# A two-layer decoder trunk: layer 0's output projection by seven products, and what makes room for it

## The chip, the core and the metric

The kernel runs on one core of a Trainium2 chip. The core has a matrix engine (TensorE, PE in the profile), a vector engine (VectorE, DVE), a scalar engine (ScalarE, ACT), GpSimd (POOL) and SyncE (SP, which here only issues transfers). Each engine works through a queue of its own in order; semaphores make one wait for another. Transfers (DMA) between DRAM and the core's memory (SBUF) are issued from the queues of SP and POOL. Matrix products collect in PSUM, eight banks of 128 partitions x 512 floats. The metric is the device time of one execution in microseconds (us).

## The reference

Two layers on x, 512 positions by 2048 channels, all in float32:

```python
for l in range(DEPTH):                                   # 2
    mod = c_act @ w_mod[l] + b_mod[l]                    # modulation: 3 x 2048 numbers
    shift, scale, gate = jnp.split(mod, 3, axis=-1)
    h = rmsnorm(x, norm_gain[l]) * (1.0 + scale) + shift
    proj = h @ w_in[l]                                   # 2048 x 7504
    ...
    y_a = sparse_attention(q_a, k_a, v_a, ...) * silu(g_a)     # 8 heads, softmax
    y_b = head_groupnorm(retention(q_b, k_b, v_b)) * silu(g_b) # 8 heads
    y = jnp.concatenate([y_a, y_b], axis=-1) @ w_out[l]        # 2048 x 2048
    x = x + gate * y
```

## The kernel before

Channels lie on the partitions: x, h and y are 16 tiles of 128 channels by 512 positions. Every float32 operand of a product is split into a high and a low part, and a product is three matmuls (high-high, high-low, low-high), in lines L390 to L398 for plain groups.

**The stream.** All products are cut into groups, and each group into chunks of 512 KB of weights: a load `wf` on SP's queue, a copy to the high part `wh` on ScalarE (L324), a subtraction to the low part `wl` on VectorE (L334), and then the chunk's matmuls. `step` (one call a chunk) issues the load five chunks ahead and the split two chunks ahead of the matmuls, then the group's `pre` work, some steps of modulation, side work of attention and retention, and the chunk's own matmuls. A scheduler then sets the order on each engine; engines and SP's queue keep that order when the kernel runs, whatever comes late.

The groups of a layer, in order: S and the indexer, VB, QK (four), QA (two), GA (two), GB (two), and the output projection. In layer 0 the projection is four plain groups OUT of 512 output channels each, eight chunks of 24 matmuls of 512 columns (`pj<-y`). Their results are evacuated by L1461 (gate times result plus x, on VectorE; x comes in by the loads `xr`), squared on ScalarE and added up on VectorE (L556, L557), since the next layer begins with a norm. The fourth group's last two chunks run by halves of the positions (`out_halves`, tiles `po`), so that the sums of squares (`prs`, L1505) and layer 1's first `h` come early.

In layer 1 the projection already runs in four groups O7 by **seven products** (L1335 to L1365): a 2 x 2 block product, of 256 channels and 256 positions a block, in seven block products instead of eight. A chunk is 42 matmuls of 256 columns. This takes sums of weight blocks (`wsum`, split into `ws` or `wsh` and `wsl`, L272 to L291) and sums of blocks of y (`put_seven`). The results `u1`, `u3`, `uc` of a group are scaled by the gate on ScalarE (L1389), then POOL adds x with an accumulating transfer (L1398) and stores the sum to the output (L1399); the fourth block goes another way (`xr`, L1404 and L1411). POOL issues them in order: accumulate, store, accumulate, store, accumulate, store.

**Modulation.** Layer 0's gate and layer 1's modulation are computed on the side (`mod_rest`), in half-tile steps: a load `mw` of 512 KB, a tiny copy on POOL from the newest `wl` (L416; it only holds the step back until that split is done), and a multiply-and-sum on VectorE (L417). Two `mw` tiles take turns. `MODN` is the number of steps a chunk in each group. Layer 1's scale and shift must be there before layer 1 begins. 96 steps lie before that.

Of the kernel before, what the change touches and what calls it, by code (L numbers as in the profile page):

```python
# [136 lines left out]
def hybrid_trunk(ctx, tc, xt, positions, wmod, w_in, w_out, cst_d, dec_d, out):  # L137
# [128 lines left out]
    def seven_hi(i):  # L266

        if "sum" not in seven:
            seven["sum"] = sm("wsum", D, tag="cb")
# [2 lines left out]
        act(h[:, :3 * QC], w[:, QC:], AF.Copy)  # L272
        tt(s[:, :2 * QC].rearrange("p (b c) -> p b c", c=QC), w[:, :QC].unsqueeze(1).to_broadcast([P, 2, QC]),
           w[:, 2 * QC:].rearrange("p (b c) -> p b c", c=QC), op=OP.subtract)
# [1 line left out]
        tt(s[:, 3 * QC:], w[:, QC:2 * QC], s[:, 2 * QC:3 * QC], op=OP.subtract)
        if i % 3 < 2:
            t = gen_mw("ws", F32R)
            pieces = [(t[:, :1024], t[:, 1024:], slice(0, 1024))]
        else:  # L280
            pieces = [(G("wsh", F32R), G("wsl", F32R), slice(n * T, (n + 1) * T)) for n in range(2)]
        for sh, _, c in pieces:
            act(sh, s[:, c], AF.Copy)
        whl[i] = h, s, pieces

    def seven_lo(i):
        h, s, pieces = whl[i]
        lo = ring.tile([P, 1024], F32R, name="wl", tag="wl")
        tt(lo[:, :3 * QC], wf.pop(i)[:, QC:], f(h[:, :3 * QC]), op=OP.subtract)
        for sh, sl, c in pieces:  # L290
            tt(sl, s[:, c], f(sh), op=OP.subtract)  # L291

        def part(q):
            if q < 3:
                return h[:, q * QC:(q + 1) * QC], lo[:, q * QC:(q + 1) * QC]
            c0 = (q - 3) * QC
            sh, sl, c = next(p for p in pieces if p[2].start <= c0 < p[2].stop)
            o = c0 - c.start
            return sh[:, o:o + QC], sl[:, o:o + QC]
# [186 lines left out]


# [456 lines left out]
    def layer(l):  # L944
# [285 lines left out]
        def att_task(h, qh, ql):  # L1230
# [48 lines left out]
            for j in range(NB):  # L1279
                v, su = Lt[j]  # L1280
                ts(v, v, su, None, op0=OP.mult)
# [109 lines left out]
        def seven_put(g, i, t, v):  # L1391
# [7 lines left out]
            (dma if g.end else nc.gpsimd.dma_start)(out=xs_of(outv, g, i, t), in_=halves(v))  # L1399

# [55 lines left out]

        def evac_out(g):
            def ev(n, ps):
                k = 4 * g + n
                t = A(k, "xn") if first else G("xo")  # L1460
                stt(t, ps, mod_col(l, 2, k), xr.pop(k), op0=OP.mult, op1=OP.add)  # L1461
                if first:
                    X[k] = t
                    if k == 0:
                        ss["t"] = G("ssq")
                    if k < KT - 4:
                        add_sq(ss["t"], t, k)
# [177 lines left out]
```

## Time and profile before

| what | value |
|---|---|
| median of 3 runs | 1850.31 us (1849.68 to 1850.46) |
| the profiled execution, its time | 1849.68 us |
| its span in the profile | 1847.9 us |
| VectorE, ScalarE busy | 1384.4 us, 888.0 us |
| layer 0's projection, first to last plain matmul and on to `po` | 783.06 to 946.33 us |
| layer 1's projection begins | 1681.14 us |
| modulation steps (L417), both layers | 132 of 1.2 to 1.5 us |

The page gives busy time, the clock that was granted to TensorE, and the chain of work that ended last. In rows of groups, the last part is the idle time of the engine just ahead of the group, and what ended it. In a timeline a row is start, duration, engine, line, operation, and in brackets the idle time before it and what ended that. Layer 0's projection lies at slices 17 to 20 of the page's 40.

### The profile page before, as it was taken

How to read it: one execution, taken by the hardware profiler on the slowest of the kernel's cores; microseconds unless marked ns; L12 is line 12 of the kernel's file. 1: busy time of each engine (PE TensorE's matmuls, PEld its weight loads, DVE VectorE, ACT ScalarE, POOL GpSimd, SP SyncE). 2: the span in 40 equal slices, each digit the busy share in tenths (PEclk: the TensorE clock that was granted, in tenths of full speed). 3: DMA queues.
4: the chain of work that ended last, by engine and by line, in shares of the span. 5: the costliest groups of instructions: out<-in, count | busy, mean ns of one | idle time of the engine just before them, and what ended most of it. 6: DMA issues, size and time to landing. Idle time of an engine off the chain costs nothing.

```text
span 1847.9 us, 26300 instructions
## 1 busy us (share of the span) xinstructions
PE 1821.7 (99%) x9644; PEld 1562.9 (85%) x9644; DVE 1384.4 (75%) x2438; ACT 888.0 (48%) x1708; POOL 70.8 (4%) x184
## 2 busy tenths in 40 slices
PE   7999999999999999999999999999999999999998
PEld 7878888888888888888899988888888888889998
DVE  7996699787867846777776699377875686369886
ACT  7668943564546532422235542344444554245443
POOL 0001000000000000100000000000000000000111
PEclk7999999999999999999999999999999999999999
DMA  9995533333454547789864323444534354333554
GB/s 371 364 321 178 165 88 92 109 114 95 123 186 123 174 147 236 233 281 308 304 208 129 103 80 100 142 124 147 155 120 124 93 185 135 102 92 109 149 151 130
DMA packets 175762, 304.55 MB, mean 165 GB/s; under 512 B 16960, under 2 KB 92864, under 8 KB 172048
## 3 DMA queue, kind: packets, MB, share of 16 engines
q1 hardware_dynamic: 171328, 295.23, 50.5%
q0 software_dynamic: 4160, 7.41, 1.6%
q8 instruction: 76, 1.25, 0.3%
q14 instruction: 54, 0.44, 0.1%
q10 hardware_dynamic: 144, 0.22, 0.0%
HBM read 289.18 MB, written 13.63 MB: 164 GB/s over the span
## 4 chain that ended last, share of the span: by engine, by line
PE 83%; DVE 2%; ACT 2%; DMA 1%; issue 1%; SPq 0%; DVEq 0%; ACTq 0%
PE pj L390 15%; PE pj L391 15%; PE pj L392 15%; PE pj L398 6%; PE pj L397 6%; PE pj L396 6%; PE p L1356 3%; PE p L1355 3%; PE p L1354 3%; PE ptr L177 1%; PE pdot L1028 1%; DVE wl L334 1%; PE pdot L1030 1%; ACT wh L324 1%; PE plg L1250 1%
## 5 line engine op out<-in xcount | busy, mean ns | idle before, releaser
L324 ACT ACTIVATE wh<-wf 128x1024 fp32r<-128x1024 f32 (+2 forms) x277 | 284.7, 1029 | 586.9 <-PE pj L391 390.1
L334 DVE TENSOR_TENSOR wl<-wf,wh 128x1024 fp32r<-128x1024 f32 (+2 forms) x277 | 326.6, 1180 | 289.1 <-ACT wh L324 282.5
L390 PE MATMUL pj<-h,wh 128*128 128x512 f32 (+1 forms) x1280 | 488.4, 382 | 1.9 <-ACT bt L911 1.7
L391 PE MATMUL pj<-h,wh 128*128 128x512 f32 (+1 forms) x1280 | 485.9, 380 | 2.6 <-DVE h L631 2.6
L392 PE MATMUL pj<-h,wl 128*128 128x512 f32 (+1 forms) x1280 | 485.7, 379 | 0.5 <-DVE wl L334 0.5
L390 PEld LDWEIGHTS pj<-h,wh 128*128 128x128 f32 x1280 | 240.6, 188 | 44.9 <-issue 2.5
L391 PEld LDWEIGHTS pj<-h,wh 128*128 128x128 f32 x1280 | 240.6, 188 | 42.1 <-DVE h L631 3.8
L392 PEld LDWEIGHTS pj<-h,wl 128*128 128x128 f32 x1280 | 240.5, 188 | 41.4 <-DVE wl L334 1.1
L396 PE MATMUL pj<-wh,h 128*128 128x512 f32 (+1 forms) x616 | 234.6, 381 | 4.1 <-ACT h L625 3.4
L397 PE MATMUL pj<-wl,h 128*128 128x512 f32 (+1 forms) x616 | 233.6, 380 | 0.7 <-DVE wl L334 0.7
L398 PE MATMUL pj<-wh,h 128*128 128x512 f32 (+1 forms) x616 | 232.6, 380 | 0.2 <-DVE h L631 0.2
L396 PEld LDWEIGHTS pj<-wh,h 128*128 128x128 f32 x616 | 116.5, 189 | 26.7 <-ACT h L625 3.9
L397 PEld LDWEIGHTS pj<-wl,h 128*128 128x128 f32 x616 | 116.5, 189 | 20.3 <-DVE wl L334 1.1
L398 PEld LDWEIGHTS pj<-wh,h 128*128 128x128 f32 x616 | 116.2, 189 | 20.4 <-DVE h L631 0.4
L417 DVE CUSTOM_DVE_ANT_0 mw<-mw,cb 128x1024 f32<-128x1024 f32 (+1 forms) x64 | 93.0, 1453 | 7.0 <-POOL mp L416 5.6
L417 DVE CUSTOM_DVE_ANT_0 mw<-mw,cb,mp 128x1024 f32<-128x1024 f32 x68 | 88.3, 1298 | 12.4 <-POOL md L416 7.9
L392 PE MATMUL pj<-y,wl 128*128 128x512 f32 x240 | 93.4, 389 | 0.0
L391 PE MATMUL pj<-y,wh 128*128 128x512 f32 x240 | 93.4, 389 | 0.0
L390 PE MATMUL pj<-y,wh 128*128 128x512 f32 x240 | 93.4, 389 | 0.0
L1262 ACT ACTIVATE bias<-bias,mx 128x128 f32<-128x128 f32 (+1 forms) x64 | 35.9, 561 | 65.3 <-DVE mx L1261 64.6
L1036 DVE SCALAR_TENSOR_TENSOR iacc<-relu,wi,iacc 128x384 f32<-128x384 f32 (+2 forms) x96 | 55.5, 613 | 10.1 <-ACT relu L1034 7.2
L894 ACT ACTIVATE ind<-pos,pt 128x512 bf16<-128x512 f32 (+3 forms) x128 | 61.4, 553 | 0.1
(549 smaller groups left out, 3077.3 us busy)
## 6 DMA issues: line engine op xcount, KB each, us to landing
wf<-in_w_in_dram SPq DMA_DIRECT2D x155, 512.0 KB, 3.7
mw<-in_wmod_dram SPq DMA_DIRECT2D x136, 512.0 KB, 5.7
wf<-in_w_in_dram SPq DMA_DIRECT2D x136, 256.0 KB, 3.1
mw<-in_wmod_dram SPq DMA_DIRECT2D x28, 1024.0 KB, 8.6
wf<-in_w_out_dram SPq DMA_DIRECT2D x32, 512.0 KB, 5.3
wf<-in_w_out_dram SPq DMA_DIRECT2D x64, 256.0 KB, 3.5
dec<-in_decay_dram SPq DMA_DIRECT2D x32, 256.0 KB, 4.0
xT<-in_xt_dram SPq DMA_DIRECT2D x16, 256.0 KB, 5.4
```

What stands on the lines that cost most here:

```text
L324: act(h[:, :n], wf[i][:, :n], AF.Copy)
L334: tt(lo[:, :n], wf.pop(i)[:, :n], f(whl[i][:, :n]), op=OP.subtract)
L390: mm(q, wh[:, o:o + P], ah, start=s0, stop=False)
L391: mm(q, wh[:, o:o + P], al, start=False, stop=False)
L392: mm(q, wl[:, o:o + P], ah, start=False, stop=s1)
L396: mm(q, ah[:, n * P:(n + 1) * P], wh[:, o:o + g.N], start=s0, stop=False)
L397: mm(q, ah[:, n * P:(n + 1) * P], wl[:, o:o + g.N], start=False, stop=False)
L398: mm(q, al[:, n * P:(n + 1) * P], wh[:, o:o + g.N], start=False, stop=s1)
L417: nc.vector.tensor_tensor_reduce(w[:, lo:hi], w[:, lo:hi], cb[:, lo:hi], scale=ng(l, k, 1) if q == 1 else 1.0, scalar=init, op0=OP.mult, o ...
L894: act(v, tab["pos"][:, :w], AF.Sign, bias=tab["pt"][:, col:col + 1], scale=-1.0)
L1036: stt(a[:, :w], r[:, :w], L["WI"][:, c0:c0 + 1], a[:, :w], op0=OP.mult, op1=OP.add)
L1354: mm(dst[m], wh[:, c], bh, start=k == 0 and (own or m == 0), stop=False)
```

## The change

1. Layer 0's first three groups (`NW = 3`) become seven-product groups like layer 1's. y is needed both plain (for the fourth group) and in sums, so `put_both` makes both. Results go to `xs_d[1]`, the next layer's input, by POOL's accumulates and stores (now L1470, L1471). They are squared later, in `squares()`, called at the third chunk of the next group, and loaded back into the tiles X during the fourth group (`RELOAD`, L1535, on SP). Weight sums in layer 0 stand in tiles `s0`, `s1`.
2. Modulation moves ahead of the projection: 84 of the 96 steps are done by the end of the first GB group (`MODSTOP`, 42 tiles); the last 12 begin with the fourth group (`mod_on`). In the groups: QK2 2, QK3 8, QA 20, GA 10 and 21, GB 23 and 0, projection 12; before: QA 8, GA 16, GB 24, OUT the rest.
3. The softmax probabilities are divided by their sums on ScalarE instead of VectorE (L1281, now L1330), in both layers.
4. The fourth group and what follows use the other PSUM banks (`SWAP`).

```diff
+NW = 3
+SWAP = NW % 2
+MODN = [{"QK2": 0.25, "QK3": 1.0, "QA": 1.25, "GA0": 1.25, "GA1": 2.625, "GB0": 2.875, "OUT": 2.5}, {**{f"QK{g}": 0.5 for g in range(4)}, "GA0": 1.0, "GA1": 1.0}]
+MODSTOP = 42
+RELOAD = {0: (0, 1, 2), 1: (3, 4, 5), 2: (6, 7), 3: (8, 9), 4: (10, 11)}
...
+        big = stream[i][0].l == 1
+        if big:
+            if "sum" not in seven:
+                seven["sum"] = sm("wsum", D, tag="cb")
+            o = i % 2 * 1024
+            s = [seven["sum"][:, o + n * T:o + (n + 1) * T] for n in range(2)]
+        else:
+            s = [G(f"s{n}") for n in range(2)]
...
-            next(modgen, None)
+            if st["modon"] or st["modn"] < 2 * MODSTOP:
+                st["modn"] += 1
+                if DEBUG:
+                    print("mod", st["modn"], i, g.name, ch)
+                next(modgen, None)
...
-            if j < len(REST):
+            if j < len(REST) and (j < MODSTOP or st["modon"]):
                 if lo == 0:
                     tiles[j] = MW()
                 dma(tiles[j][:, lo:lo + D // 2], wmod[2 * KT + j][:, lo:lo + D // 2])
+
+        def resume():
+            st["modon"] = True
+            for lo in (0, D // 2):
+                load(MODSTOP, lo)
+        state["resume"] = resume
...
+    def mod_on():
+        state["resume"]()
+        st["mod"] = -MODN[0]["OUT"]
...
+    def put_both(p, y0, y1):
+
+        a, b = slice(0, QC), slice(QC, 2 * QC)
+        t13, t24 = G("t13"), G("t24")
+        tt(t13[:, a], y0[:, b], y0[:, a], op=OP.subtract)
+        tt(t13[:, b], y0[:, b], y1[:, b], op=OP.add)
+        tt(t24[:, a], y1[:, b], t13[:, a], op=OP.add)
+        tt(t24[:, b], y1[:, a], t24[:, a], op=OP.subtract)
+        put_y(2 * p, y0)
+        put_y(2 * p + 1, y1)
+        names = {}
+        for k, keys in ((2 * p, ("B11", "B12")), (2 * p + 1, ("B21", "B22"))):
+            for key, c in zip(keys, (a, b)):
+                names[key] = Hh[k][:, c], Hl[k][:, c]
+        for keys, src, hi, lo in ((("T1", "T3"), t13, G("e1", F32R), G("e3", F32R)),
+                                  (("T2", "T4"), t24, A(2 * p, "eh", F32R), A(2 * p + 1, "el", F32R))):
+            act(hi, src, AF.Copy)
+            tt(lo, src, f(hi), op=OP.subtract)
+            for key, c in zip(keys, (a, b)):
+                names[key] = hi[:, c], lo[:, c]
...
-                ts(v, v, su, None, op0=OP.mult)
+                act(v, v, AF.Copy, scale=su)
...
-                put_seven(p, Y.pop(2 * p), Y.pop(2 * p + 1))
+                (put_both if first else put_seven)(p, Y.pop(2 * p), Y.pop(2 * p + 1))
...
-        outv = out.rearrange("(k p) t -> k p t", p=P)
+        outv = xs_d[1] if first else out.rearrange("(k p) t -> k p t", p=P)
+        sq_todo = deque()
+
+        def squares():
+
+            while sq_todo:
+                t, v = sq_todo.popleft()
+                c = HALF[t]
+                if not ss:
+                    ss["t"] = G("ssq")
+                s = ss["t"][:, c]
+                if t not in ss:
+                    ss[t] = True
+                    act(s, v[:, :QC], AF.Square)
+                    parts = (1,)
+                else:
+                    parts = (0, 1)
+                q = G("sq")
+                o = QC * parts[0]
+                act(q[:, o:], v[:, o:], AF.Square)
+                for m in parts:
+                    tt(s, s, q[:, m * QC:(m + 1) * QC], op=OP.add)
 
         def pre_seven(g):
             def pre(ch):
+                if ch == 2:
+                    squares()
...
             (dma if g.end else nc.gpsimd.dma_start)(out=xs_of(outv, g, i, t), in_=halves(v))
+            if first:
+                sq_todo.append((t, v))
...
+                    if g == NW:
+                        mod_on()
+                if g == NW:
+                    if ch == 2:
+                        squares()
+                        if NW == 3:
+                            act(sm("dummy", 1), ss["t"][:, :1], AF.Sqrt)
+                    for k in RELOAD.get(ch, ()):
+                        X[k] = A(k, "xn")
+                        dma(X[k], xs_d[1][k])
...
-                    ps = psum.tile([P, T], F32, name="po", tag=("px", "pj")[hf])[:, :nh]
+                    ps = psum.tile([P, T], F32, name="po", tag=("px", "pj")[hf ^ SWAP])[:, :nh]
...
+        for n in range(NW if first else 4):
+            g = Group(W_out, [(512 * n, 512)], 2, "7", 4, hact, None, name="O7")
+            g.by_ch = {ch: seven_chunk for ch in range(g.nch)}
+            if n == 3:
+                g.by_ch[g.nch - 1] = lambda i: None
+            g.pre = pre_seven(g)
+            g.idx, g.end, g.u, g.fin, g.l = n, n == 3, {}, {}, l
+            seq.append(g)
...
+            seq += [Group(W_out, [(512 * g, 512)], 2, "t", 4, hact, evac_out(g), pool="px", pre=pre_out(g), name="OUT")
+                    for g in range(NW, 3)]
+            seq += [Group(W_out, [(1536, 512)], 2, "t", 4, hact, evac_out(3), pool=("pj", "px")[SWAP], pre=pre_out(3), name="OUT", kr=(0, KT - 4)),
+                    Group(W_out, [(1536, 512)], 2, "t", 4, hact, None, name="OUT", kr=(KT - 4, KT))]
```

How this moves instructions, at three places. First ScalarE in the projection's third group. Before, from the second OUT group on (`wh<-wf` are the weight copies of chunks, `sq<-xn` squares of the previous group's results):

```order
L324 ACTIVATE wh<-wf 128x1024 x7
L556 ACTIVATE sq<-xn 128x512
L324 ACTIVATE wh<-wf 128x1024
L556 ACTIVATE sq<-xn 128x512 x3
L324 ACTIVATE wh<-wf 128x1024 x7
```

In the change, in the third group (`wh`, `ws`, `wsh` are copies of a chunk's weights and weight sums; `uc`, `u_8834`, `u_8850` and `xr` are the four results of the second group, the first three of which come back from POOL's accumulates in this order):

```order
L277 ACTIVATE wh<-wf 128x768
L299 ACTIVATE ws<-s_9033 128x512
L1444 ACTIVATE sq<-uc 128x512
L299 ACTIVATE ws<-s_9034 128x512
L1444 ACTIVATE sq<-u_8834 128x512
L1444 ACTIVATE sq<-u_8850 128x512
L1444 ACTIVATE sq<-xr 128x512
L277 ACTIVATE wh<-wf 128x768
L299 ACTIVATE wsh<-s_9108 128x512
```

The squares of all four results now stand ahead of the weight copy of chunk 5 (the `wh` behind `sq<-xr`); before, a square waited for VectorE's evacuation alone.

Second VectorE in the fourth group. Before, from the last addition of the third group's squares on (`mw` rows are modulation steps, two for each tile, followed by the read of their sum):

```order
L557 TENSOR_TENSOR ssq<-ssq,sq 128x512
L417 ISA mw,mp<-mw,cb 128x1024
L417 ISA mp 128x1
L334 TENSOR_TENSOR wl<-wf,wh 128x1024
L417 ISA mw,md_90<-mw,cb,mp 128x1024
L417 ISA md_90 128x1
L334 TENSOR_TENSOR wl<-wf,wh 128x1024
L417 ISA mw,mp<-mw,cb,cst 128x1024
L417 ISA mp 128x1
L417 ISA mw,md_90<-mw,cb,mp,cst 128x1024
L417 ISA md_90 128x1
L334 TENSOR_TENSOR wl<-wf,wh 128x1024
```

In the change, from the `wl` of chunk 3 on (the row `wl` near the end is chunk 4's):

```order
L348 TENSOR_TENSOR wl<-wf,wh 128x1024
L1446 TENSOR_TENSOR ssq<-ssq,sq 128x256 x3
L435 ISA mw,mp<-mw,cb 128x1024
L435 ISA mp 128x1
L1446 TENSOR_TENSOR ssq<-ssq,sq 128x256
L435 ISA mw,md_90<-mw,cb,mp 128x1024
L435 ISA md_90 128x1
L348 TENSOR_TENSOR wl<-wf,wh 128x1024
L1446 TENSOR_TENSOR ssq<-ssq,sq 128x256
L435 ISA mw,mp<-mw,cb,cst 128x1024
L435 ISA mp 128x1
L1446 TENSOR_TENSOR ssq<-ssq,sq 128x256
```

The additions of squares, which wait for POOL's transfers and ScalarE's squares, and the first modulation steps stand ahead of chunk 4's `wl`. All twelve steps follow from here to the end of the group, with four `wl` among them.

Third POOL and SP in the fourth group of the change; before, POOL had only the copies `<-wl` here. POOL (`xs_83` is the next layer's input in DRAM, `u_9343` and `u_9359` are results of the third group):

```order
L1470 DMA u_9343<-in_xt_dram 128x2x256
L1471 DMA xs_83<-u_9343 128x2x256
L1470 DMA u_9359<-in_xt_dram 128x2x256
L1471 DMA xs_83<-u_9359 128x2x256
L434 COPY mp<-wl 128x1
L434 COPY md_90<-wl 128x1
L434 COPY mp<-wl 128x1
L434 COPY md_90<-wl 128x1
```

SP (`xn<-xs_83` are the reloads, `mw` the modulation loads, `wf` weight chunks):

```order
L490 DMA mw<-in_wmod_dram 128x1024 x2
L327 DMA wf<-in_w_out_dram 128x2x512
L1535 DMA xn<-xs_83 128x512 x4
L490 DMA mw<-in_wmod_dram 128x1024 x2
L327 DMA wf<-in_w_out_dram 128x2x512
L490 DMA mw<-in_wmod_dram 128x1024 x3
```

The copies that let the modulation steps go stand behind the last store of the third group, which waits for the accumulate before it. On SP the reload of the third group's four tiles, which waits for the stores, stands ahead of the later loads `mw` and of weight chunks.

More of the change, by code (lines that the diff above doesn't have):

```diff
@@ L165, in PX, with PB @@
         return psum.tile([P, T], F32, name=name, tag="px")
+    def PB(name):
+        return psum.tile([P, T], F32, name=name, tag=("px", "pj")[SWAP])
     def A(i, name, dt=F32):
@@ L266, in seven_hi @@
     def seven_hi(i):
-        if "sum" not in seven:
-            seven["sum"] = sm("wsum", D, tag="cb")
-        w, s = wf[i], seven["sum"][:, i % 2 * 1024:(i % 2 + 1) * 1024]
+        w = wf[i]
         h = ring.tile([P, 1024], F32R, name="wh", tag="wh")
         act(h[:, :3 * QC], w[:, QC:], AF.Copy)
-        tt(s[:, :2 * QC].rearrange("p (b c) -> p b c", c=QC), w[:, :QC].unsqueeze(1).to_broadcast([P, 2, QC]),
+        big = stream[i][0].l == 1
[6 more added lines that the diff above has]
+            s = [G(f"s{n}") for n in range(2)]
@@ L277, in seven_hi @@
         if i % 3 < 2:
             t = gen_mw("ws", F32R)
-            pieces = [(t[:, :1024], t[:, 1024:], slice(0, 1024))]
+            hl = [(t[:, n * T:(n + 1) * T], t[:, 1024 + n * T:1024 + (n + 1) * T]) for n in range(2)]
         else:
[L281 to L284, printed above, removed]
+            hl = [(G("wsh", F32R), G("wsl", F32R)) for n in range(2)]
@@ L286, in seven_lo @@
+        pieces = [(sh, sl, v) for (sh, sl), v in zip(hl, s)]
+        if big and i % 3 < 2:
+            pieces = [(t[:, :1024], t[:, 1024:], seven["sum"][:, o:o + 1024])]
+        for sh, _, v in pieces:
+            act(sh, v, AF.Copy)
+        whl[i] = h, pieces, hl
     def seven_lo(i):
-        h, s, pieces = whl[i]
+        h, pieces, hl = whl[i]
         lo = ring.tile([P, 1024], F32R, name="wl", tag="wl")
         tt(lo[:, :3 * QC], wf.pop(i)[:, QC:], f(h[:, :3 * QC]), op=OP.subtract)
-        for sh, sl, c in pieces:
-            tt(sl, s[:, c], f(sh), op=OP.subtract)
+        for sh, sl, v in pieces:
+            tt(sl, v, f(sh), op=OP.subtract)
@@ L295, in part @@
                 return h[:, q * QC:(q + 1) * QC], lo[:, q * QC:(q + 1) * QC]
[L296 to L299, printed above, removed]
+            o = (q - 3) % 2 * QC
+            return tuple(v[:, o:o + QC] for v in hl[(q - 3) // 2])
         whl[i] = h, lo, part
@@ L1412, in seven_fin @@
             dma(outv[k][:, t * QC:(t + 1) * QC], r[:, c])
+            if first and m:
+                sq_todo.append((t, r))
         def seven_out(g, prod):
@@ L1459, in ev @@
                 k = 4 * g + n
[L1460 to L1467, printed above, removed]
+                X[k] = A(k, "xn")
+                stt(X[k], ps, mod_col(l, 2, k), xr.pop(k), op0=OP.mult, op1=OP.add)
+                if k < KT - 4:
+                    add_sq(ss["t"], X[k], k)
                     if k == KT - 5:
                         act(sm("dummy", 1), ss["t"][:, :1], AF.Sqrt)
-                    if k < KT - 4:
-                        dma(xs_d[1][k], t)
-                else:
-                    dma(out[k * P:(k + 1) * P, :], t)
+                    dma(xs_d[1][k], X[k])
             return ev
@@ L1501, in out_halves @@
                         dma(xs_d[1][k], t)
-                pss, r = PX("prs"), sm("rcol2", 2, bufs=2)
+                pss, r = PB("prs"), sm("rcol2", 2, bufs=2)
                 for m, v in enumerate((ss["t"][:, c], q[1][:, :nh], q[1][:, nh:])):
@@ L1518, in layer @@
         gs = []
-        S = Group(W_in, [(KA, 256), (KI, 80)], 2, "tok", 4, hact, evac_s, pre=None if first else pre_l1, name="S")
+        S = Group(W_in, [(KA, 256), (KI, 80)], 2, "tok", 4, hact, evac_s, pool="px" if SWAP and not first else "pj", pre=None if first else pre_l1, name="S")
         part = {}
@@ L1587, in layer @@
-        if first:
-            seq += [Group(W_out, [(512 * g, 512)], 2, "t", 4, hact, evac_out(g), pre=pre_out(g), name="OUT")
-                    for g in range(4)]
-        else:
-            for n in range(4):
-                g = Group(W_out, [(512 * n, 512)], 2, "7", 4, hact, None, name="O7")
-                g.by_ch = {ch: seven_chunk for ch in range(g.nch)}
-                if n == 3:
-                    g.by_ch[g.nch - 1] = lambda i: None
-                g.pre = pre_seven(g)
-                g.idx, g.end, g.u, g.fin = n, n == 3, {}, {}
-                seq.append(g)
@@ L1599, in layer @@
-        if first:
-            seq[-1:] = [Group(W_out, [(1536, 512)], 2, "t", 4, hact, evac_out(3), pre=pre_out(3), name="OUT", kr=(0, KT - 4)),
-                        Group(W_out, [(1536, 512)], 2, "t", 4, hact, None, name="OUT", kr=(KT - 4, KT))]
+                      post=post_seven if g == 1 else None, name=f"GB{g}") for g in range(2)]
+        for n in range(NW if first else 4):
[6 more added lines that the diff above has]
+            seq.append(g)
```

21 lines of the change are left out of this document (9 added, 12 removed).

## The prediction

> **What bounds the kernel now.** I read the page first (busy shares, clock, the chain that ended last), then the matmuls' start times, then the groups and timelines of the stages that the change touches.
>
> ```profile
> PE 1821.7 (99%) x9644; PEld 1562.9 (85%) x9644; DVE 1384.4 (75%) x2438; ACT 888.0 (48%) x1708; POOL 70.8 (4%) x184
> PEclk7999999999999999999999999999999999999999
> PE 83%; DVE 2%; ACT 2%; DMA 1%; issue 1%; SPq 0%; DVEq 0%; ACTq 0%
> L390 PE MATMUL pj<-y,wh 128*128 128x512 f32 x240 | 93.4, 389 | 0.0
> ```
>
> TensorE is busy 99% of the span at the full clock except at the very start, it holds 83% of the chain, and the matmuls of layer 0's output projection (pj<-y) never waited: 0.0 in the last column. So a matmul that goes saves its pitch, and any other work costs nothing until it makes TensorE wait. The whole prediction is therefore one subtraction and a search for new waits.
>
> The subtraction comes from matmul starts (columns: start, duration, engine, line):
>
> ```profile
> 783.06 0.39 PE L390 MATMUL pj<-y,wh 128*128 128x512 f32 x1
> ...
> 946.33 0.28 PE L1491 MATMUL po<-y,wh 128*128 128x256 f32 x1
> ```
>
> ```profile
> 1681.14 0.28 PE L1354 MATMUL p<-y,wh 128*128 128x256 f32 x1
> ...
> 1802.09 0.28 PE L1354 MATMUL p<-y,wh 128*128 128x256 f32 x1
> ```
>
> From 783.06 to 946.33 layer 0 issues 720 matmuls of 512 columns: 226.8 ns each, 43.54 us for a group of 192. From 1681.14 to 1802.09 layer 1 runs three seven-product groups, 1008 matmuls of 256 columns: 120.0 ns each, 40.32 us a group. (Half of 226.8 would be 113.4; the halves don't run at half the pitch, and I use 120.)
>
> **Part 1: three groups by seven products.** Removed: 3 x 43.54. Added: 3 x 40.32. **Gain 9.7 us**, if nothing new waits. The dearer preparation (two subtractions and two splits more per chunk) runs two chunks, 10 us, ahead of TensorE, as it does in layer 1, where the three groups above follow each other without a gap; I take it at nothing. If that lead were lost, each chunk's splits would show, which is the next term.
>
> What layer 1 does not have is what follows the groups here. The results must become the next layer's input: POOL adds x by an accumulating transfer and stores the sum, then ScalarE squares the sums, VectorE adds up the squares, and SyncE loads the sums back. All of these stand in in-order queues ahead of things that TensorE needs. How late are they? Layer 1 shows POOL's part already (the bracket is the idle time before, and what ended it):
>
> ```profile
> 1742.80 0.74 POOL L1399 DMA_DIRECT2D out_dram<-u  x1 [3.53 <-DMA u<-xs]
> ...
> 1764.95 1.20 POOL L1398 DMA_DIRECT2D uc<-xs  x1 [21.41 <-DVE xr L1404]
> 1771.61 0.75 POOL L1399 DMA_DIRECT2D out_dram<-uc  x1 [5.46 <-DMA uc<-xs]
> 1772.35 1.23 POOL L1398 DMA_DIRECT2D u<-xs  x1
> 1779.12 0.74 POOL L1399 DMA_DIRECT2D out_dram<-u  x1 [5.54 <-DMA u<-xs]
> 1779.85 1.24 POOL L1398 DMA_DIRECT2D u<-xs  x1
> 1786.38 0.75 POOL L1399 DMA_DIRECT2D out_dram<-u  x1 [5.29 <-DMA u<-xs]
> ...
> 1827.07 0.74 POOL L1399 DMA_DIRECT2D out_dram<-u  x1 [7.49 <-DMA u<-xs]
> ```
>
> POOL issues an accumulate, waits for it to land, issues its store, then the next. The group before ended at 1761.77 (1681.14 + 2 x 40.32). The third accumulate has landed when its store can be issued, at 1786.38: **24.6 us after the group's end**. The other two groups (ends 1721.45, 1802.09) give 21.4 and 25.0. Call this L. Three rounds in series make it, so it can't shrink much: the first accumulate is issued 3.2 us after the end, and a round is some 1.2 + 5.5 + 0.75.
>
> *The seven-product groups 1 and 2 (second and third of the projection).* ScalarE's queue (the order shown above in the change) has the squares of the previous group ahead of the weight copy `wh` of chunk 5. The third sum's square waits for L, and behind it stand another square, `wh`, and the copies of the weight sums; VectorE's low parts follow.
>
> ```profile
> L272 ACT ACTIVATE wh<-wf 128x768 fp32r<-128x768 f32 x24 | 20.2, 841 | 38.3 <-PE p L1355 25.0 <-issue 12.8 <-ACT ws L283 0.5
> L283 ACT ACTIVATE wsh<-wsum 128x512 fp32r<-128x512 f32 x16 | 9.9, 627 | 17.9 <-DVE wsum L273 12.0 <-DVE wsum L276 5.9
> ...
> L289 DVE TENSOR_TENSOR wl<-wf,wh 128x768 fp32r<-128x768 f32 x24 | 22.8, 953 | 6.3 <-ACT wh L272 6.1
> L291 DVE TENSOR_TENSOR wsl<-wsum,wsh 128x512 fp32r<-128x512 f32 x16 | 10.6, 684 | 0.3
> ```
>
> ```profile
> L556 ACT ACTIVATE sq<-xn 128x512 f32<-128x512 f32 x7 | 4.4, 633 | 2.3 <-DVE xn L1461 2.0
> ```
>
> (The first four rows are of layer 1's groups, the last is layer 0's square of the same shape; after a bar stand busy us, mean ns, and the idle time before.) So `wl` is ready at L + 0.63 + 0.63 + 0.84 + 0.95 = L + 3.05. TensorE begins chunk 5 at 5 x 5.04 = 25.2 after the group's start and reads `wl` with its third matmul, at 25.4. Late by 0 (L = 21.4: 24.4), 2.2 (24.6), 2.6 (25.0). The low part of the first weight sum comes at L + 3.4 and is read at about 26.2: late by 0 to 2.3 by that path. I take the middle group's **2.2 us for each of two groups, 4.4 in sum; bounds 0 and 5.7** (2.9 each if both sums wait one copy more). Later chunks are not later still, since VectorE is not full in such a group:
>
> ```profile
> 1721.40:1761.80 40.40, 40.40 (x339) 40.40 (x339) 33.05 (x52) 19.02 (x29) 5.92 (x6) 1.00 0.59 157
> ```
>
> (Columns: stretch, length, busy PE, PEld, DVE, ACT, POOL with their instructions, clock, DMA share, GB/s.)
>
> **Part 2: modulation.** The steps moved ahead go into stages whose VectorE has room. The tightest is the first GB group, with 23 steps instead of 12:
>
> ```profile
> 696.00:739.50 43.50, 43.50 (x193) 36.04 (x192) 26.23 (x36) 10.76 (x12) 2.74 (x12) 1.00 0.75 241
> 826.60:870.10 43.50, 43.50 (x194) 36.03 (x192) 30.65 (x41) 10.69 (x12) 2.46 (x13) 1.00 0.91 309
> ```
>
> VectorE: 26.23 + 11 x 1.3 = 40.5 of 43.5. Transfers: 8 weight chunks and 23 half tiles of 0.52 MB make 16.3 MB. The second row moves 309 GB/s at share 0.91, so 340 at share 1, and 16.3 MB takes 48 us: up to 4.4 us late at the stage's end, inside the two chunks (10.9 us) that the weights run ahead. I take 0; bounds 0 and 4.4.
>
> The 12 steps left for the last group are what costs. POOL writes a gate for each step, a copy of the newest `wl`; that instruction now stands on POOL behind the store of the third sum. And on VectorE these steps stand *ahead* of `wl` of chunks 4 and 5 and of both last chunks, and of all that leads to the matmuls `prs` (the sum of squares). Before, POOL had no transfer in layer 0, and the steps lay spread between the chunks. The durations, from the groups of the last OUT group up to `prs`:
>
> ```profile
> L334 DVE TENSOR_TENSOR wl<-wf,wh 128x1024 fp32r<-128x1024 f32 x6 | 7.3, 1222 | 6.0 <-ACT wh L324 6.0
> L417 DVE CUSTOM_DVE_ANT_0 mw<-mw,cb,mp 128x1024 f32<-128x1024 f32 x5 | 6.6, 1319 | 0.9 <-DMA mw<-in_wmod_dram 0.4 <-POOL md L416 0.3
> L1461 DVE SCALAR_TENSOR_TENSOR xn<-pj,md,xr 128x512 f32<-128x512 f32 x7 | 4.9, 742 | 0.0
> L417 DVE CUSTOM_DVE_ANT_0 mw<-mw,cb 128x1024 f32<-128x1024 f32 x3 | 3.7, 1221 | 0.3 <-POOL mp L416 0.3
> ...
> L417 DVE CUSTOM_DVE_ANT_0 mw<-mw,cb,cst 128x1024 f32<-128x1024 f32 x2 | 2.6, 1284 | 0.6 <-POOL mp L416 0.6
> L1495 DVE SCALAR_TENSOR_TENSOR xn<-po,md,xn 128x256 f32<-128x256 f32 x3 | 1.4, 479 | 0.0
> L1499 DVE TENSOR_TENSOR ssq<-ssq,sq 128x256 f32<-128x256 f32 x2 | 0.9, 426 | 0.2
> L334 DVE TENSOR_TENSOR wl<-wf,wh 128x672 fp32r<-128x672 f32 x1 | 0.8, 849 | 0.0
> ```
>
> ```profile
> 952.09 0.50 PE L1505 MATMUL prs<-cst,ssq 128*128 128x1 f32 x4
> ```
>
> TensorE now reaches `prs` at 952.09, 38.4 us after the group's start (913.67 = 783.06 + 3 x 43.54), without a wait. In the changed order VectorE does, from the first step on: 12 steps x 1.29 (the mean of the ten rows' 12.9) = 15.5; four `wl` x 1.22 = 4.9; three adds of squares x 0.43 = 1.3; four `xn<-pj` x 0.74 = 3.0; the short `wl` 0.85; three `xn<-po` 1.4; two adds 0.9; some 0.2 for the column add: **28.0 us**. The first step can start when POOL has issued the third store and the gate: L + 0.75 + 0.3, that is 22.4, 25.7 or 26.0. So `prs` comes at 50.4 to 54.0; with the median 53.7 it is **15.3 us late; bounds 12.0 and 15.6**. (`wl` of chunk 4 alone is late by 8 us on the way: 25.7 + 4.2 against 21.8. That wait lies inside the 15.3.)
>
> *SyncE in the same group.* The reloads of the third group's sums (L1535) stand ahead of later `mw` and `wf` loads, and wait for the stores.
>
> ```profile
> DMA to landing us min/median/max: 4.4/5.3/8.3
> ...
> DMA to landing us min/median/max: 2.3/3.1/5.6
> ```
>
> ```profile
> mw<-in_wmod_dram SPq DMA_DIRECT2D x136, 512.0 KB, 5.7
> ```
>
> The first row is for L1398, the accumulates, the second for L1399, the stores. The third store lands at about 25.4 + 3.1 = 28.5, and an `mw` load behind it at 34.2. VectorE wants that tile for its fifth step, at 25.7 + 4 x 1.29 + 2 x 0.43 + 1.22 = 32.9. **1.0 us; bounds 0 and 3.**
>
> *The clock.* TensorE will idle for some 4 us just ahead of `prs` (its last `po` ends near 49, `prs` comes at 53.7).
>
> ```profile
> 34.47 0.42 PE L396 MATMUL pj<-wh,h 128*128 128x336 f32 x1 [3.39 <-ACT h L625]
> ```
>
> ```profile
> 35.00:39.00 4.00, 3.85 (x15) 3.81 (x15) 4.00 (x6) 1.03 (x2) 0.55 (x1) 0.57 1.15 363
> ```
>
> After an idle 3.39 us the next 4 us were granted 0.57: 0.43 x 4 = **1.7 us; bounds 0 and 3.4** (a second such idle). [...]
>
> **Parts 3 and 4.**
>
> ```profile
> L1281 DVE TENSOR_SCALAR bias<-bias,su 128x128 f32<-128x128 f32 (+1 forms) x64 | 24.2, 381 | 0.8
> ```
>
> 64 scalings leave VectorE (24.2 us) for a ScalarE that is 48% busy. No matmul wait hangs on them, so 0; bounds -1 and +1 (0.8 is the idle time before them). The other banks: the last group showed no wait for a bank, 0.
>
> **Sum**: -9.7 + 4.4 + 15.3 + 1.0 + 1.7 = **+12.7 us**. It is made against the profiled run, 1849.68 (span 1847.9, the lowest of three and 0.6 below the median): **1862.4**. All bounds at their lower ends: -9.7 + 12.0 = +2.3, 1852. At their upper ends for the terms of the projection: -9.7 + 5.7 + 15.6 + 3 + 3.4 = +18, 1867.7.
>
> **The rivals.**
>
> *The other side: the sums land in time, and only the gain is left.* The change is faster when the first step of the last group can start before 20.1 us: then -9.7 + 20.1 + 28.0 - 38.4 = 0. At 10.4 all is hidden: 1840.0. For it: layer 0's transfers go at a time when no modulation loads run. Against: POOL's three rounds were 22.4 at best in layer 1, and there too no modulation was loaded. **0.14** for 1840 to 1846.
>
> *About no change*: L near its lowest end, squares hidden, clock not gated, 1850 to 1853. **0.14**.
>
> *POOL's transfers are later than in layer 1*, since the last groups share the queues with reloads and stores. At the longest landing of the row above, 8.3 instead of 5.3, three rounds add 9 us to L, and with it to the last group: 1871. [...] **0.05**.
>
> *Modulation ahead overruns*: GB's 4.4 us show after all: 1867. **0.05**.
>
> *Forecast*, 1853.5 to 1868 around 1862.4: **0.62**.
>
> **How the numbers follow.** About 0.2%, 3.7 us, is what a measurement of this kernel can tell from no change. Faster 0.14; same (1846 to 1854) 0.14; slower 0.62 + 0.05 + 0.05 = 0.72. A range from 1849 to 1869 leaves out the faster case and the late transfers, about 0.19.
>
> **What would show it.** In the changed profile: matmuls p<-y in layer 0 at 120 ns; a TensorE wait of 1 to 3 us near chunk 5 of the second and third group, ended by ScalarE's `wh` behind `sq`; in the last group a first L435 step some 25 us after its start, a TensorE wait of about 8 us on `wl` at chunk 4 and one at `prs`, the group some 15 us longer. Wrong it would be if POOL's third store in layer 0 is issued before 19 us, or if the first L435 steps run ahead of it.

## The result and the profile after

The changed kernel takes **1876.45 us** (median of 4, 1875.66 to 1876.84) against 1850.38 for the kernel before in the same comparison: ratio 1.0141, 95% interval 1.0125 to 1.0157. It is slower by 26 us where 12.7 were forecast, and outside the range. The profiled execution took 1875.66 us, span 1873.9.

The page after, in the lines that answer to those of before:

```profile
PE 1828.3 (98%) x10076; PEld 1581.8 (84%) x10076; DVE 1444.3 (77%) x2568; ACT 955.3 (51%) x1865; POOL 89.4 (5%) x202
PEclk7999999999999999999989999999999999999999
PE 44%; DVE 2%; DMA 2%; ACT 1%; issue 1%; SPq 0%; POOL 0%; DVEq 0%; ACTq 0%
```

TensorE is busy 6.6 us *longer*, though the seven products save 9.7 us of matmuls, and the rest of the 26 us is idle time. A stretch of the clock row has fallen to 8. So matmuls have become slower somewhere, and TensorE waits somewhere. Where, is read best from the first matmul of each stage in the two traces (us from the span's start):

| stage begins | before | after | later by |
|---|---|---|---|
| first GB group | 696.02 | 698.83 | 2.8 |
| second GB group | 739.54 | 743.42 | 3.9 |
| projection, group 1 | 783.06 | 793.54 | **10.5** |
| group 2 | 826.58 | 835.97 | 9.4 |
| group 3 | 870.10 | 876.29 | 6.2 |
| group 4 | 913.67 | 919.57 | 5.9 |
| layer 1's first QI group | 992.02 | 1014.67 | **22.7** |
| layer 1's projection | 1681.14 | 1706.64 | 25.5 |
| span | 1847.9 | 1873.9 | 26.0 |

The three seven-product groups took 42.43, 40.32 and 43.28 us; against 40.32 they lost 2.1, 0 and 3.0. The stretch from group 4 to layer 1's QI took 95.1 instead of 78.35: 16.8 more. Ahead of the projection 10.5 were lost, behind layer 1's QI 3.3. Together: 10.5 - 9.7 + 5.1 + 16.8 + 3.3 = 26.0.

TensorE's waits, first of the kernel before, then of the changed one, from 340 to 1060 us (what waited, for what; us in total, times, longest). Before, the longest entry of all is

```profile
PE pvar L1173 <- ACT rsqh L1169: 1.0, 2, 0.6
```

and after, the seven longest:

```profile
PE prs L1579 <- DVE ssq L1573: 5.3, 1, 5.3
PE pj L408 <- ACT silu L1376: 4.6, 2, 3.7
PE pj L410 <- DVE wl L348: 2.4, 1, 2.4
PE p L1405 <- DVE wl L305: 2.0, 2, 1.2
PE po L1567 <- DVE wl L348: 1.5, 1, 1.5
PE p L1403 <- ACT wsh L299: 1.2, 2, 0.8
PE pj L408 <- ACT wh L338: 1.0, 1, 1.0
```

`prs`, `po`, `wh` and the `wl` of L348 belong to the last group, the `p` rows to the seven-product groups. The second row belongs to the second GB group, where no loss was forecast.

**The last group.** POOL's timeline after:

```profile
899.54 0.75 POOL L1471 DMA_DIRECT2D xs<-u  x1 [3.90 <-DMA u<-in_xt_dram]
920.68 1.20 POOL L1470 DMA_DIRECT2D uc<-in_xt_dram  x1 [20.39 <-ACT uc L1461]
928.87 0.74 POOL L1471 DMA_DIRECT2D xs<-uc  x1 [6.99 <-DMA uc<-in_xt_dram]
929.60 1.23 POOL L1470 DMA_DIRECT2D u<-in_xt_dram  x1
935.12 0.75 POOL L1471 DMA_DIRECT2D xs<-u  x1 [4.29 <-DMA u<-in_xt_dram]
935.86 1.24 POOL L1470 DMA_DIRECT2D u<-in_xt_dram  x1
940.64 0.74 POOL L1471 DMA_DIRECT2D xs<-u  x1 [3.55 <-DMA u<-in_xt_dram]
941.37 0.20 POOL L434 COPY mp<-wl 128x1 f32<-128x1 f32 x1
```

and VectorE's:

```profile
941.00 0.43 DVE L1446 TENSOR_TENSOR ssq<-ssq,sq 128x256 f32<-128x256 f32 x1 [4.65 <-ACT sq L1444]
941.61 1.23 DVE L435 CUSTOM_DVE_ANT_0 mw<-mw,cb 128x1024 f32<-128x1024 f32 x1 [0.19 <-POOL mp L434]
...
944.30 1.22 DVE L348 TENSOR_TENSOR wl<-wf,wh 128x1024 fp32r<-128x1024 f32 x1
...
964.33 1.29 DVE L435 CUSTOM_DVE_ANT_0 mw<-mw,cb,cst 128x1024 f32<-128x1024 f32 x1 [1.77 <-DMA mw<-in_wmod_dram]
```

The third store goes out 21.1 us after the group's start, the gate follows it, and the first step begins at 22.0; chunk 4's `wl`, wanted at 21.8, begins at 24.7, and the last `mw` load makes the eleventh step wait. TensorE reaches `prs` at 972.50, 52.9 us after the group's start instead of 38.4: 14.5 late, the rest of the 16.8 comes behind it.

On the way TensorE waited twice at chunk 4, with only two matmuls between, and then ran at a lower clock (columns of the second view: stretch, length, busy PE, PEld, DVE, ACT, POOL, clock, DMA share, GB/s):

```profile
942.48 0.50 PE L408 MATMUL pj<-y,wh 128*128 128x512 f32 x1 [0.96 <-ACT wh L338]
945.58 0.79 PE L410 MATMUL pj<-y,wl 128*128 128x512 f32 x1 [2.37 <-DVE wl L348]
```

```profile
919.90:952.50 32.60, 29.27 (x116) 23.29 (x115) 15.60 (x26) 10.61 (x16) 6.73 (x11) 0.90 0.87 259
```

The clock of 0.90 is 3.3 us over this stretch. It adds nothing to the 14.5, since TensorE then waits 5.3 us at `prs` for VectorE in any case.

**The second GB group.** The stretches of the two GB groups after, and the second one before (length, busy PE, PEld, DVE, ACT, POOL, clock, DMA share, GB/s):

```profile
698.80:743.40 44.60, 43.71 (x193) 35.85 (x191) 34.52 (x49) 9.49 (x11) 4.96 (x21) 1.00 0.86 296
743.40:793.50 50.10, 46.40 (x192) 37.87 (x193) 48.43 (x85) 25.41 (x41) 2.49 (x3) 0.93 0.48 161
```

```profile
739.50:783.00 43.50, 43.50 (x193) 36.03 (x193) 34.04 (x49) 17.54 (x25) 6.58 (x12) 1.00 0.73 242
```

The second group took 6.6 us longer: 3.7 idle, and 2.9 because the same 192 matmuls ran at a clock of 0.93. Its wait, on TensorE and on ScalarE:

```profile
751.48 0.80 PE L408 MATMUL pj<-h,wh 128*128 128x512 f32 x1 [3.68 <-ACT silu L1376]
```

```profile
749.88 1.06 ACT L338 ACTIVATE wh<-wf 128x1024 fp32r<-128x1024 f32 x1 [5.54 <-DMA wf<-in_w_in_dram]
750.85 0.58 ACT L1376 ACTIVATE silu<-pj 128x512 f32<-128x512 f32 x1
```

TensorE wants the PSUM bank of the first group's fourth result. ScalarE's `silu` empties it, and stands behind the copy `wh` of a chunk that is needed two chunks later, and whose weights have not arrived. So a late load costs at once, although its chunk is not yet due. Why it is late, SyncE's queue shows, from 690 to 752 us, before and after:

```profile
SPq L313 <- DVE wl L334: 36.7, 11, 5.0
SPq L472 <- DVE md L417: 13.8, 8, 3.4
```

```profile
SPq L490 <- DVE md L435: 38.8, 13, 5.1
SPq L327 <- DVE wl L348: 10.7, 4, 5.3
```

Before, the queue mostly waits to load weights (L313) until a weight buffer is free: weights are as early as their ring allows. After, it mostly waits to load modulation (L490) until VectorE has used up one of the two `mw` tiles, and the weights stand behind that.

### The profile page after: what moved, and what is told of

It reads as the page before. It is cut to its first block, busy times and chain, and to the rows that moved or that the text cites. A ratio compares the mean times of both kernels' runs of the same rounds, so it can differ in the third digit from the quotient of the medians.

```text
span 1873.9 us, 27622 instructions
## 1 busy us (share of the span) xinstructions
PE 1828.3 (98%) x10076; PEld 1581.8 (84%) x10076; DVE 1444.3 (77%) x2568; ACT 955.3 (51%) x1865; POOL 89.4 (5%) x202
## 4 chain that ended last, share of the span: by engine, by line
PE 44%; DVE 2%; DMA 2%; ACT 1%; issue 1%; SPq 0%; POOL 0%; DVEq 0%; ACTq 0%
PE pj L409 7%; PE pj L408 7%; PE pj L410 7%; PE pj L416 3%; PE pj L415 3%; PE pj L414 3%; PE p L1403 3%; PE p L1404 3%; PE p L1405 3%; DMA mw<-in_wmod_dram 1%; PE pdot L1077 1%; DMA wf<-in_w_out_dram 1%; PE ptr L184 0%; DVE wl L348 0%; PE pdot L1079 0%
## 5 line engine op out<-in xcount | busy, mean ns | idle before, releaser
L338 ACT ACTIVATE wh<-wf 128x1024 fp32r<-128x1024 f32 (+3 forms) x253 | 258.7, 1024 | 463.2 <-PE pj L409 249.2
L348 DVE TENSOR_TENSOR wl<-wf,wh 128x1024 fp32r<-128x1024 f32 (+3 forms) x253 | 297.1, 1175 | 206.6 <-ACT wh L338 204.9
L277 ACT ACTIVATE wh<-wf 128x768 fp32r<-128x768 f32 x56 | 46.9, 839 | 51.5 <-PE p L1404 33.3
L1405 PE MATMUL p<-y,wl 128*128 128x256 f32 x224 | 63.6, 284 | 2.0 <-DVE wl L305 2.0
L435 DVE CUSTOM_DVE_ANT_0 mw<-mw,cb,cst 128x1024 f32<-128x1024 f32 (+1 forms) x32 | 56.0, 1749 | 11.4 <-DMA mw<-in_wmod_dram 10.8
L1085 DVE SCALAR_TENSOR_TENSOR iacc<-relu,wi,iacc 128x384 f32<-128x384 f32 (+2 forms) x96 | 55.6, 614 | 10.5 <-ACT relu L1083 7.6
L1404 PE MATMUL p<-y,wh 128*128 128x256 f32 x224 | 63.3, 283 | 0.0
L1403 PE MATMUL p<-y,wh 128*128 128x256 f32 x224 | 63.3, 283 | 0.0
```

The costliest lines, as they stand in the source:

```text
L338: act(h[:, :n], wf[i][:, :n], AF.Copy)
L348: tt(lo[:, :n], wf.pop(i)[:, :n], f(whl[i][:, :n]), op=OP.subtract)
L435: nc.vector.tensor_tensor_reduce(w[:, lo:hi], w[:, lo:hi], cb[:, lo:hi], scale=ng(l, k, 1) if q == 1 else 1.0, scalar=init, op0=OP.mult, o ...
L1403: mm(dst[m], wh[:, c], bh, start=k == 0 and (own or m == 0), stop=False)
L1404: mm(dst[m], wh[:, c], bl, start=False, stop=False)
L1405: mm(dst[m], wl[:, c], bh, start=False, stop=stop)
```

## The experiments

Each is compared with the kernel before on its chip (medians 1850.55 to 1850.79). The changed kernel's 1876.45 is from another set of runs, with 1850.38 for the kernel before.

**Modulation ahead alone.** The kernel before with the new rates, the stop after 84 steps and `mod_on` in the last group:

```diff
-MODN = [{"QA": 0.5, "GA": 1.0, "GB": 1.5, "OUT": 1.65}, ...
+MODN = [{"QK2": 0.25, "QK3": 1.0, "QA": 1.25, "GA0": 1.25, "GA1": 2.625, "GB0": 2.875, "OUT": 2.5}, ...
+MODSTOP = 42
...
+                    if g == 3:
+                        mod_on()
```

> The kernel before with the modulation moved ahead alone (84 steps by the end of GB0, 12 in the last group; plain projection). Theory A, the transfers of GB0 can't carry 23 half tiles beside the weights, so weight chunks come late in GB0 and GB1: the projection starts 8 to 11 us later than in the kernel before (783.06), in all 1858 to 1863 us. Rival B, the 10.5 us by which the changed kernel's projection starts late come from the splits of y in GB1 and the scaling on ScalarE: then this one stays within 1849 to 1853 us.

Measured 1856.42 (1855.48 to 1858.11), ratio 1.0031, interval 1.0018 to 1.0044. The profiled execution begins its projection at 789.49, 6.4 late, and its second GB group waits for `silu` 3.1 us. So modulation alone makes a good part of the loss; A's sign and place hold, its size was set too high, and the time lies between the ranges of A and B. The other 4.1 of the 10.5 are not taken apart: 1.7 of them are there when the first GB group begins, ahead of the splits of y, and in the three runs below that keep these rates and change only what comes later (No gate, Squares later, Additions), the projection began 6.1, 4.2 and 8.1 us late. From the last group's start to layer 1's QI this kernel takes 79.0 us, 0.7 more than before: **12 steps in the last group, where the kernel before has ten, are no burden in themselves.**

**Scaling on ScalarE alone.**

```diff
-                ts(v, v, su, None, op0=OP.mult)
+                act(v, v, AF.Copy, scale=su)
```

> The kernel before with the softmax scaling moved to ScalarE alone. Theory A, it costs nothing and the changed kernel's losses in the attention stages and in layer 1 (3.9 us before GB1, 2.9 us in layer 1's QK groups) come with the other parts: 1849.5 to 1851.5 us. Rival B, the scaling stands in ScalarE's queue ahead of copies that TensorE needs and makes these losses: 1853 to 1857 us.

Measured 1850.52, ratio 1.0001, interval 0.9991 to 1.0010: A. This part costs and brings nothing here.

**No gate in the last group.** The changed kernel without POOL's copy for its 12 steps there:

```diff
-        if "gate" in state:
+        if "gate" in state and not 2 * MODSTOP < st["modn"] <= 2 * MODSTOP + 12:
```

> The changed kernel with the POOL copy left out for the 12 steps of the last group (the copy only holds a step back, no result changes). VectorE's order then has four steps ahead of the adds of squares. Theory A, the last group is late because POOL's stores hold the steps and VectorE runs them in series after them: four steps of 1.3 us leave the chain, 1870 to 1872.5 us. Rival B, the squares alone hold VectorE (they wait for the same transfers) and the steps fit into its pauses: no change, 1875 to 1877 us.

Measured 1870.26 (1869.03 to 1873.73), 6.2 below the changed kernel. VectorE's timeline in the last group, which here begins at 918.01:

```profile
920.05 1.22 DVE L435 CUSTOM_DVE_ANT_0 mw<-mw,cb 128x1024 f32<-128x1024 f32 x1
...
936.35 0.42 DVE L1446 TENSOR_TENSOR ssq<-ssq,sq 128x256 f32<-128x256 f32 x1 [6.07 <-ACT sq L1444]
936.69 1.28 DVE L435 CUSTOM_DVE_ANT_0 mw<-mw,cb,cst 128x1024 f32<-128x1024 f32 x1
```

Two steps leave the chain at once; the next ones still stand behind additions of squares. In the profiled executions the stretch to layer 1's QI shrinks by 3.6 us (91.5 instead of 95.1), while the projection also began 4.4 us earlier. So the gate is one part of the hold, the squares the other, and both wait for the same transfers. That the time falls into A's range is partly luck: not four steps left the chain but two, and the last group also began 1.6 us earlier, which the edit does not explain.

**Squares later.** `if ch == 2` becomes `if ch == 4` in both places that call `squares()`.

> The changed kernel with the squares of groups 0 and 1 asked for at the fifth chunk instead of the third; on ScalarE they then stand behind the weight copy of chunk 5 (second group) and of chunk 6 (third group); in the last group the order of squares stays as it was. Theory A, the third group loses about 3 us because chunk 5's copy waits behind squares: its length falls from 43.3 to 40.3 us and the time to 1873 to 1874 us. Rival B, the wait comes from the late splits of weight sums on VectorE or from weight transfers: 1876 to 1877 us.

Measured 1874.22 (1872.47 to 1876.48), 2.2 less and a little above A's range. The single runs of the two kernels overlap, so the time alone decides nothing, but the trace does: the third group takes 40.32 us instead of 43.28. Its 3.0 us were the squares ahead of chunk 5's weight copy, as A said. In this execution the projection began 6.3 earlier, the first group took 46.05, 3.6 longer, and from the last group's start to layer 1's QI it took 97.7 instead of 95.1 (the squares are asked for later there too). The loss around the second GB group moves between executions, and hides part of such a gain.

**Additions on VectorE.** Layer 0's results get their x there, from a load made earlier, as layer 1's last group does; SyncE stores them:

```diff
-                    for i, t in (...) if g.end else ((0, 1),):
+                    for i, t in (...) if g.end or first else ((0, 1),):
...
-            if g.end:
+            if g.end or first:
                 r = res.pop((i, t))
                 tt(v, v, r, op=OP.add)
...
-            (dma if g.end else nc.gpsimd.dma_start)(...)
+            (dma if g.end or first else nc.gpsimd.dma_start)(...)
```

> The changed kernel with x added to layer 0's results on VectorE (from an earlier load) and the sums stored from SyncE's queue, as layer 1's last group does; POOL has no transfers in layer 0, the 12 steps and their gates stay. Theory A, the last group is late because everything in it waits some 21 us for the third accumulate: sums are there some 5 us after a group's end, the last group (from its start to S) takes 16.8 us longer than before now and 0 to 5 then; the third group's 3 us go as well: 1858 to 1863 us. Rival B, the 12 steps and the loads behind the reloads are simply too much work for the last group wherever they begin: it stays 10 us or more late, 1868 to 1873 us.

Measured **1857.28** (1854.35 to 1860.85), 19.2 less than the changed kernel: A. VectorE's first and last step of the last group, which began at 919.49:

```profile
927.71 1.23 DVE L435 CUSTOM_DVE_ANT_0 mw<-mw,cb 128x1024 f32<-128x1024 f32 x1
...
954.88 1.34 DVE L435 CUSTOM_DVE_ANT_0 mw<-mw,cb,mp 128x1024 f32<-128x1024 f32 x1
```

The first begins 8.2 us after the group's start instead of 22.0, and the stretch to layer 1's QI is 81.0 us, 2.7 more than before instead of 16.8. The steps, the gates and the reloads are all still there; only what they waited for is gone. The third group takes 40.32 us here. The first takes 47.66, because TensorE waits in it for a split of weights (the row below), at a mean clock of 0.93. This was the slowest execution of the seven (1860.85), and with the wider spread as well (Both, below) that group takes 40.6 us.

```profile
PE p L1405 <- DVE wl L305: 4.2, 1, 4.2
```

**Modulation spread.** The same 84 steps ahead, but 14 instead of 23 in the first GB group:

```diff
-MODN = [{"QK2": 0.25, "QK3": 1.0, "QA": 1.25, "GA0": 1.25, "GA1": 2.625, "GB0": 2.875, "OUT": 2.5}, ...
+MODN = [{"VB1": 0.5, "QK2": 0.25, "QK3": 1.0, "QA": 1.5, "GA0": 1.375, "GA1": 2.75, "GB0": 1.75, "OUT": 2.5}, ...
...
-        seq += [... name="VB") for g in range(2)]
+        seq += [... name=f"VB{g}") for g in range(2)]
```

> The changed kernel with the same 84 steps ahead spread wider: 4 in the second VB group, 24 instead of 20 in QA, 11, 22 and 14 in GA0, GA1 and GB0 instead of 10, 21 and 23. Theory A, GB0's 23 half tiles delay the weights of GB0 and GB1: the projection starts 1 to 4 us later than in the kernel before instead of 4 to 10, and the time falls to 1867 to 1872 us. Rival B, GB1's own work (the splits of y on VectorE, 48 of 50 us busy) makes the delay: the projection's start and the time stay, 1874 to 1877 us.

Measured 1865.35 (1862.7 to 1868.27), 11.1 less than the changed kernel, 1.7 below A's range. The projection begins at 785.63, 2.6 late, and the stretches of the two GB groups are without idle time:

```profile
698.60:742.10 43.50, 43.50 (x193) 36.03 (x192) 33.91 (x47) 10.76 (x13) 2.48 (x13) 1.00 0.83 282
742.10:785.60 43.50, 43.50 (x193) 36.04 (x192) 40.18 (x72) 26.96 (x42) 0.00 (x0) 1.00 0.33 97
```

SyncE's queue, 690 to 752 us, is back to waiting for weight buffers most:

```profile
SPq L327 <- DVE wl L348: 29.1, 10, 5.0
SPq L490 <- DVE md L435: 19.0, 8, 5.1
```

The splits of y are in the second GB group here too, without a loss: without late weights they fit. The third group and the stretch from the last group to layer 1's QI still lose (42.2 and 95.8 us), as they should: nothing was done about POOL's transfers here.

**Both.**

> Both edits, VectorE's additions and the wider spread. Theory A, the two losses are independent and nothing else takes their place: the gain of 9.7 us of the seven products remains less 4 to 9 us of small waits, 1846 to 1853 us. Rival B, the losses cover each other or VectorE becomes the bound in the groups: 1857 us or more.

Measured **1847.36** (1844.84 to 1851.96), ratio 0.9982, interval 0.9972 to 0.9991: faster than the kernel before. The two edits bring 19.2 and 11.1 alone and 29.1 together, so they are two losses, nearly independent. From 780 to 990 us one wait is left in the view of TensorE's waits:

```profile
PE prb L1585 <- DVE rcol L1582: 0.2, 1, 0.2
```

The groups take 40.3 to 40.6 us, and layer 1's QI begins 6.0 us earlier than before, of 9.7 possible; 3.2 were lost ahead of the projection.

**The rest: layer 1, and layer 0 ahead of GA.** The rows that show layer 1's loss in the changed kernel, VectorE in a QK group and TensorE's waits from 1000 to 1720:

```profile
1362.94 0.69 DVE L1183 TENSOR_TENSOR s<-psc,dec 128x512 f32<-128x512 f32 x1 [1.19 <-DMA dec<-in_decay_dram]
```

```profile
PE pvar L1222 <- ACT rsqh L1218: 1.0, 1, 1.0
```

Two kernels tried to get these back, and a third had both edits. In layer 1's rates, `"QI": 0.0625` makes one step more:

> As e8_both, with one modulation step more in layer 1's QI groups, so that the later loads of modulation stand elsewhere on SyncE's queue: before, a weight chunk's two loads stood between the mw pair and the decay matrix dec (L1112); in the changed kernel dec (L1161) stands right behind the mw pair, and now weight loads stand between them again. Theory A, layer 1's 2.9 us come from dec landing late behind mw (6.4 us instead of 4.0), so that the retention's copies and the matmuls pvar come late: layer 1 runs as in the kernel before, 1843.5 to 1845.5 us. Rival B, they come from the scaling on ScalarE or from chance in the scheduler's order: 1847 us or more.

Layer 0 with `{"VB1": 0.75, "QA": 1.5, "GA0": 1.5, "GA1": 3.0, "GB0": 2.25, "OUT": 2.5}`:

> As e8_both, with no modulation in layer 0's QK groups: 6, 24, 12, 24 and 18 steps in VB1, QA, GA0, GA1, GB0. Theory A, the 2 to 3 us that are lost before GA0 come from modulation in QK3 (the same dec loads, and VectorE), and 18 half tiles in GB0 still fit: 1844 to 1846 us. Rival B, GB0 is over its limit again with 18: 1849 us or more.

> Both edits of e9_phase and e10_no_mod_in_qk. If both losses are what theory A of those says, 1841 to 1844 us, about 0.4% below the kernel before; if one of them is not, 1844 to 1848 us.

The first gave 1848.22 (ratio 0.9984, 0.9975 to 0.9992), no better than 1847.36 and where B put it. In its profiled execution the waits at `pvar` in layer 1 are gone, and from QI to the projection layer 1 takes 690.1 us instead of 692.0 (before: 689.1), but the time did not follow. So the place of the `dec` load explains those waits in this trace; that it is worth 2.9 us of time is *not shown*. The second gave 1854.30 (1847.71 to 1860.12; ratio 1.0019, 1.0009 to 1.0030), the third 1852.41 (ratio 1.0010, 1.0002 to 1.0019), above both of its ranges. In the second, the projection began at 784.5, 1.8 earlier than in the combined kernel and without a loss in the two GB groups, but its first group then took 46.9 us, 6.3 more, at a clock of 0.93 behind this wait:

```profile
PE p L1405 <- DVE wl L305: 3.3, 1, 3.3
```

So modulation in QK costs some 1 to 2 us (without it the first GB group began at 697.5 and 697.7, with it and the wider spread at 698.6 to 699.7). The new rates are too much in another place, as rival B has it; SyncE's queue again waits for `mw` tiles most (34.3 us against 11.6 for weights, 690 to 752 us). That the 18 steps in the first GB group do it, and not the 24 in the second GA group or the others, is likely but *not shown*; with the rates of the spread, 14 there, no such wait is left.

## Why the prediction was wrong

**The gain, 9.7 us: right.** The second seven-product group took exactly 40.32 us, and in the combined kernel so did two of three.

**Squares ahead of chunk 5's copy, 4.4 us for two groups: right in mechanism, 3.0 in size.** L was 23.3 us for the third group (899.54 - 876.29), and it lost 3.0; moving the squares gave that back. By the working, 23.3 would have cost only 0.9: TensorE also waited 0.8 for the weight sums (`wsh`), a path that the working puts at 0.5 for this L. For the second, L was some 20.7 and nothing was lost. The first group's 2.1 us were not forecast; its waits, in the view above, are splits that come late from the second GB group.

**The last group, 15.3 + 1.0 + 1.7 = 18.0 us: right, 16.8.** The third store came 21.1 us after the start where 24.6 was taken as the middle of layer 1's three. That alone takes 3.5 off; some of it came back in waits for `mw` loads behind the reloads (put at 1.0, where the working's own figures give 34.2 - 32.9 = 1.3; the three longest are 4.0 together) and in the clock. So the path is right, and that the sum comes so close is partly luck. The wait on `wl` at chunk 4, put at about 8 us, was 2.4, with 1.0 for `wh` just ahead of it. Taking the transfers' wait away, and leaving the steps, removed 14.1 of the 16.8.

**The clock, 1.7 us: right in kind, too small and in two places too few.** After the 5.3 us at `prs` the stretch shows 0.83:

```profile
973.00:990.00 17.00, 16.75 (x108) 16.41 (x108) 10.56 (x28) 7.83 (x18) 1.64 (x6) 0.83 0.43 135
```

That is 0.17 x 17 = 2.9 us, and the second GB group's 0.93 cost another 2.9 where no idle time was forecast. The third place is chunk 4 of the last group, whose 3.3 us were hidden.

**The step that failed: "I take 0; bounds 0 and 4.4" for the modulation moved ahead.** By the projection's start 10.5 us were lost, and in its first group 2.1 more. Moved ahead alone, the modulation cost 6.4 of them; with the steps spread wider, the projection starts 2.6 late and its first group loses 0.3. The working took DMA throughput as the limit and set the two chunks by which weights run ahead against it. Both halves were wrong. The transfers ran at a share of 0.86 and 296 GB/s, below the 0.91 that carried 309 GB/s in the kernel before, and the run with 18 steps in the first GB group moved 321 GB/s there at 0.94 without a loss in that group. What was full was the turn of two `mw` tiles, and SyncE's queue in order behind it, which the waits of SP above show. And the two chunks cover only the matmuls of that chunk: on ScalarE the waiting `wh` stood ahead of a `silu` that TensorE needed at once. A rival with this place, but with throughput as its cause, was in the text, at 1867 and a chance of 0.05; price and chance were both too low. That the two tiles set the rate, rather than the time that loads take to land there (`mw` 6.0 us, 5.3 before; `wf` 7.0, 3.8 before), is read from the waits; a third tile wasn't tried. With the 3.3 us of layer 1, and 1.4 and 1.2 less than forecast for the squares and the last group, these 12.6 us are the whole distance from 12.7 to 26.0.

**Parts 3 and 4 at nothing.** For the scaling alone, right: 1850.52. The other banks (part 4) were not run alone. Layer 1's 3.3 us were not forecast. From QI to the projection layer 1 takes 689.1 us before, 689.1 with the scaling alone, 691.1 with the modulation ahead alone and 692.0 in the changed kernel, in one execution each, so most of it seems to come with the modulation; the place of the `dec` loads explains waits there, and the cause of the lost time stays open.

## What to carry to other kernels

Ask of every wait that an edit adds which instructions stand behind it *on its own queue*, and when those are needed: "two chunks ahead" protects the load, not the `silu` behind its copy. A result that comes back from a chain of transfers (three rounds, 20 us together, here) should not stand ahead of splits on an in-order engine; adding x on VectorE from an early load, 0.7 us each, was worth 19 us. Before moving work into a stage with "room", look at the queue that feeds it, in the view of SyncE's waits, not at the sum of bytes.

## What was not expected of the hardware

An idle time of 3.7 us in the second GB group was followed by slower matmuls (granted clock 0.50 from 751.4 to 755 us, 0.77 from there to 759, then 1.00) worth another 2.9 us, so this wait cost nearly twice what the view of waits says. After the 5.3 us at `prs` the clock was 0.50 from 973 to 976 us, 0.66 to 980, then 1.00. It need not be one long wait: at chunk 4 of the last group 0.96 and 2.37 us, two matmuls apart, were followed by a clock of 0.50 from 945 to 951 us. The short waits of the third seven-product group (none over 1.2 us) left its clock at 1.00; where between these cases it begins to fall, no run here shows:

```profile
876.30:919.90 43.60, 41.41 (x340) 40.76 (x339) 33.38 (x60) 20.63 (x37) 5.89 (x6) 1.00 0.71 211
```
